# Modulation vectors of a two-layer backbone: five chunks summed on VectorE, four chunks moved to layer 1

## The chip, the cores and the metric

The kernel runs on one core of one Trainium2 chip. The metric is the device time of one execution in microseconds; before the change it is 2871.11 us (median of 3 runs, 2866.96 to 2872.5).

## What is computed

Two layers work on 1024 latent tokens of width 1024, with 256 context tokens beside them. Every layer is steered by modulation vectors that come from a conditioning vector:

```python
s_lat = jax.nn.silu(c)
s_ctx = jax.nn.silu(c_ctx)
for layer in range(DEPTH):
    mod   = (s_lat @ ada_w[layer] + ada_b[layer])[:, None, :]
    mod_c = s_ctx @ ada_w[layer] + ada_b[layer]
    sh1, sc1, g1, sh2, sc2, g2 = jnp.split(mod, N_MOD, axis=-1)          # latents
    csh1, csc1, cg1, csh2, csc2, cg2 = jnp.split(mod_c, N_MOD, axis=-1)  # context
    h   = modulate(x, norm1_g[layer], sh1, sc1)
    h_c = modulate(ctx, norm1_g[layer], csh1, csc1)
    # layer 0: Fourier mixing and spatial gating; layer 1: neighbourhood attention
    x = x + g1 * y
    x = x + g2 * conv_ffn(modulate(x, norm2_g[layer], sh2, sc2), ...)
    # the same for ctx in layer 0 only
```

`ada_w[layer]` is 1024 x 6144 in float32. The text calls one of its twelve blocks of 1024 columns a chunk, (layer, j) with j = 0 to 5: 4 MB of weights, multiplied by one or two vectors of 1024 numbers (the streams: latents and context). Layer 1 returns the latents only, so its chunks j = 2 to 5 are needed for the latents alone; (1,0) and (1,1) are needed for both.

## The kernel before, in words

**Order of the work.** A startup computes chunks (0,1) and (0,0). The even mixer follows: twelve projections of the normed input with `even_w_in` (method `even`, helper `go`), first four for the gating values and four for the gating units, then four for the Fourier part. Then eight projections with `even_w_out` (from L1617), the ConvFFN of layer 0, the 24 projections with `odd_w_qkv` (method `qkv`, from L1105), attention, its output projection, and the ConvFFN of layer 1. A projection of 1280 columns is 8 k-steps; each k-step is three passes (a float32 product is split into high and low parts) of three matmuls, 512, 512 and 256 columns wide (L556).

**Modulation by matmuls.** `ada` (from L634) works on a chunk: for each of 8 k it loads two tiles of 128 x 512 weights (L642) into a rotation of six tiles `adaw`, and issues four matmuls (L644). The silu vectors of both streams, padded to 32 columns, are the stationary operand; four column strips of the array hold four column blocks of 256. After k = 7 VectorE copies the sums out of PSUM (L649), two transposes (L652) turn them into columns, and VectorE adds the bias (L656). `gains` (L667) makes 1 + scale times the norm's gain for j = 1 and 4.

**Modulation by sums on VectorE.** `ada_sums` (from L670) is for the latents alone: a tile of weights 128 x 512 is multiplied by a per-partition scalar of `sT` and added to an accumulator (L684 for the first k, L686 for the other seven), two halves to a chunk, two k to one load of 512 KB (L680). What is left, a sum over the partitions, is eight matmuls with a column of ones (L692), each two instructions in the profile, and one addition of the bias (L694).

**What sets the order.** Both are generators. Each `next` traces one step; hooks call it at chosen k-steps of a projection, so that a step stands in the program between two k-steps. The framework then schedules the whole program at build time: on each engine it takes the first instruction in program order that it holds to be ready. On the chip each engine runs its list in that order and waits where an operand is not there. The loads of weights go through SyncE's queue (SP), also in order.

**Where the chunks stand.** In `even`, `go(10)` takes 10 steps, `go(11)` 8 and each of `go(4)` to `go(7)` 8: chunks (0,2) to (0,5), (1,1), (1,0), all by `ada`. In the projections with `even_w_out`, a hook at every k-step takes a step of (1,2) to (1,5) by `ada_sums`; accumulator and loads share four tiles of tag `wd`. The `qkv` projections have hooks of their own: `todo` holds the head norms and transposes of the projection before, placed at k-steps 1, 3, 5 and 7, or at 2.

Of the kernel before, what the change touches and what calls it, by code (L numbers as in the profile page):

```python
# [12 lines left out]
ALU = mybir.AluOpType  # L13
# [493 lines left out]
class Net:  # L507
# [77 lines left out]
    def setup(self, pool):  # L585
# [20 lines left out]
        self.gs = self.t(cp, [P, 2, 2, 2, KD], "gs")  # L606

        def early():
# [61 lines left out]
    def ada_sums(self, layer, j, room):  # L670


        nc, a = self.nc, self.a
        acc = room()
        for half in range(2):
            x = acc[:, half * 512:half * 512 + 512]
            lo = j * D + half * 512
            for k in range(0, KD, 2):
                w = room().rearrange("p (t n) -> p t n", t=2)
                nc.sync.dma_start(w, a["ada_w"][layer, k * P:(k + 2) * P, lo:lo + 512].rearrange("(t p) n -> p t n", p=P))  # L680
                for i in range(2):
                    c = self.sT[:, k + i, 0:1]
                    if k + i == 0:
                        nc.vector.tensor_scalar(x, w[:, i], c, None, ALU.mult)  # L684
                    else:
                        nc.vector.scalar_tensor_tensor(x, w[:, i], c, x, ALU.mult, ALU.add)  # L686
                yield

        def rest():
            tr = self.t(self.ps, [P, 512], "pq")  # L690
            for e in range(KD):
                nc.tensor.matmul(tr[:, e:e + 1], acc[:, e * P:(e + 1) * P], self.ones, start=True, stop=True)  # L692
            b = layer * 48 + j * 8
            nc.vector.scalar_tensor_tensor(self.mod[:, layer, 0, j, :], tr[:, 0:KD], float(D),  # L694
                                           self.adab[:, b:b + 8], ALU.mult, ALU.add)
            self.gains(layer, j, (0,))
        return rest
# [133 lines left out]
    def even(self, h, ada, spill, ws, hooks, close):  # L831
# [34 lines left out]
        with tc.tile_pool(name="sgu", bufs=1) as pool:  # L866
# [72 lines left out]
            for g in range(G):  # L939
# [4 lines left out]
                pl, pc = go(4 + g, hooks=hk, fill=8)[0]  # L944
# [927 lines left out]
```

## Time and profile before

One execution was profiled: 2865.27 us, of which the span from its first to its last instruction is 2863.4 us. All times below are of that execution.

| | us | share of the span |
|---|---|---|
| PE (TensorE matmuls) | 2747.1 | 96% |
| PEld (weight loads of TensorE) | 2507.2 | 88% |
| DVE (VectorE) | 2247.1 | 78% |
| ACT (ScalarE) | 1375.3 | 48% |
| POOL (GpSimd) | 917.9 | 32% |

Stages that the text speaks of, by time from the span's start: `go(11)` and `go(4)` to `go(7)` from 106.5 to 236.6 us; the Fourier projections to about 361 us; the projections with `even_w_out`, in which modulation is summed, from 361 to 455 us; the `qkv` projections from 1410 to 1756 us, most of them in 1455 to 1755 us.

A row of the timeline gives start, duration, engine, line, operation and operands, the number of merged instructions, and in brackets the idle time of the engine before it and who ended it. A row of the stages gives a stretch and for each engine its busy time and, in parentheses, its instructions; then the granted TensorE clock, the share of the DMA engines, and GB/s. A line L686 is line 686 of the kernel before. A matmul's end is modelled, so the starts of weight loads (PEld), which are issued in the order of the matmuls, show the pace of TensorE best.

### The profile page before, as it was taken

How to read it: one execution, taken by the hardware profiler on the slowest of the kernel's cores; microseconds unless marked ns; L12 is line 12 of the kernel's file. 1: busy time of each engine (PE TensorE's matmuls, PEld its weight loads, DVE VectorE, ACT ScalarE, POOL GpSimd, SP SyncE). 2: the span in 40 equal slices, each digit the busy share in tenths (PEclk: the TensorE clock that was granted, in tenths of full speed). 3: DMA queues.
4: the chain of work that ended last, by engine and by line, in shares of the span. 5: the costliest groups of instructions: out<-in, count | busy, mean ns of one | idle time of the engine just before them, and what ended most of it. 6: DMA issues, size and time to landing. Idle time of an engine off the chain costs nothing.

```text
span 2863.4 us, 46977 instructions
## 1 busy us (share of the span) xinstructions
PE 2747.1 (96%) x17978; PEld 2507.2 (88%) x17978; DVE 2247.1 (78%) x3680; ACT 1375.3 (48%) x2652; POOL 917.9 (32%) x840
## 2 busy tenths in 40 slices
PE   7999999899999899999999998999989999999998
PEld 4668878799999899999888887999778999789998
DVE  4233477988998998888876666999379999889997
ACT  4221314544444444444543334999255555545454
POOL 0600014532323742222221111444355343653331
PEclk9999999899999999999999999999999999999999
DMA  8764262322223222222043325775223333333333
GB/s 309 212 195 127 80 222 90 101 84 89 75 85 95 80 82 88 75 81 88 24 145 125 142 101 158 180 180 122 63 78 104 103 96 106 109 91 102 89 104 96
DMA packets 335882, 327.63 MB, mean 114 GB/s; under 512 B 16217, under 2 KB 264617, under 8 KB 335657
## 3 DMA queue, kind: packets, MB, share of 16 engines
q1 hardware_dynamic: 331509, 315.69, 36.6%
q0 software_dynamic: 3808, 7.87, 1.0%
q8 instruction: 142, 2.33, 0.3%
q10 hardware_dynamic: 340, 1.06, 0.1%
q14 instruction: 83, 0.68, 0.1%
HBM read 277.86 MB, written 46.71 MB: 113 GB/s over the span
## 4 chain that ended last, share of the span: by engine, by line
PE 68%; DVE 20%; DMA 4%; issue 4%; ACT 2%; POOL 1%; SPq 0%; POOLq 0%; DVEq 0%; ACTq 0%
PE pq L323 20%; PE pq L556 15%; PE pq L439 12%; PE ps L556 6%; DVE xl L449 3%; DVE wh L256 3%; DVE wq L256 3%; PE pq L644 2%; DVE wd L526 2%; PE ps L565 2%; DVE g L354 2%; PE st L1284 1%; PE tl L1317 1%; DVE hx L329 1%; DVE hs L526 1%
## 5 line engine op out<-in xcount | busy, mean ns | idle before, releaser
L439 PE MATMUL pq<-act,wd 128*128 128x320 f32 (+3 forms) x3696 | 615.4, 318 | 18.6 <-DVE hx L329 6.4
L323 PE MATMUL pq<-hs,wh 128*128 128x320 f32 (+3 forms) x4128 | 609.7, 300 | 20.0 <-ACT wh L251 7.8
L323 PEld LDWEIGHTS pq<-hs,wh 128*128 128x128 f32 x4128 | 579.6, 192 | 27.6 <-ACT wh L251 9.1
L439 PEld LDWEIGHTS pq<-act,wd 128*128 128x128 f32 x3696 | 549.7, 191 | 42.8 <-DVE hx L329 8.2
L323 PE MATMUL pq<-hs,wq 128*128 128x320 f32 (+3 forms) x3144 | 470.8, 297 | 12.6 <-ACT hx L332 7.3
L556 PE MATMUL pq<-hs,wh 128*128 128x512 f32 (+3 forms) x2100 | 465.5, 356 | 3.6 <-DVE hs L802 1.9
L323 PEld LDWEIGHTS pq<-hs,wq 128*128 128x128 f32 x3144 | 437.4, 189 | 20.5 <-ACT hx L332 10.8
L556 PEld LDWEIGHTS pq<-hs,wh 128*128 128x128 f32 x2100 | 362.7, 191 | 77.5 <-issue 6.2
L248 POOL TENSOR_TENSOR ws<-wr 128x512 f32<-128x512 f32 x88 | 133.2, 1513 | 629.3 <-DMA wr<-in_ffn_w_up_dram 493.4
L449 DVE SCALAR_TENSOR_TENSOR xl<-pq,mod,xl 128x320 f32<-128x320 f32 (+5 forms) x616 | 296.1, 513 | 11.0 <-PE pq L439 10.9
L556 PE MATMUL ps<-hs,wh 128*128 128x512 f32 x840 | 242.5, 408 | 4.4 <-ACT hs L799 1.7
L256 DVE TENSOR_TENSOR wq<-wr,wq 128x512 fp32r<-128x512 f32 x246 | 226.0, 933 | 25.8 <-ACT wq L251 25.6
L332 ACT ACTIVATE hx<-pq 128x320 f32<-128x320 f32 (+3 forms) x292 | 119.2, 408 | 220.6 <-PE pq L323 214.0
L251 ACT ACTIVATE wh<-ws 128x512 fp32r<-128x512 f32 x172 | 108.3, 629 | 195.8 <-PE pq L323 173.3
L259 POOL TENSOR_TENSOR wr<-ws,wr 128x512 f32<-128x512 f32 x88 | 121.2, 1378 | 196.4 <-DVE wh L256 177.2
L556 PEld LDWEIGHTS ps<-hs,wh 128*128 128x128 f32 x840 | 143.1, 192 | 42.6 <-issue 14.4
L251 ACT ACTIVATE wq<-wr 128x512 fp32r<-128x512 f32 x262 | 162.8, 622 | 30.0 <-POOL wr L258 15.8
L329 DVE TENSOR_TENSOR hx<-hx,pq 128x320 f32<-128x320 f32 (+3 forms) x304 | 134.7, 447 | 50.1 <-PE pq L323 32.3
L256 DVE TENSOR_TENSOR wh<-ws,wh 128x512 fp32r<-128x512 f32 x172 | 157.3, 914 | 9.8 <-ACT wh L251 5.9
L1084 DVE RECIPROCAL hsq<-hsq 128x512 f32<-128x512 f32 (+1 forms) x40 | 121.1, 3030 | 53.0 <-ACT hsq L1083 52.1
L526 DVE TENSOR_TENSOR wd<-wrd,wd 128x512 fp32r<-128x512 f32 x176 | 145.3, 860 | 0.3 <-ACT wd L525 0.3
L251 ACT ACTIVATE wh<-wr 128x512 fp32r<-128x512 f32 x172 | 107.6, 625 | 76.0 <-POOL wr L259 42.4
(312 smaller groups left out, 4380.9 us busy)
## 6 DMA issues: line engine op xcount, KB each, us to landing
wr<-in_ffn_w_up_dram SPq DMA_DIRECT2D x176, 512.0 KB, 4.6
wrd<-in_ffn_w_down_dram SPq DMA_DIRECT2D x88, 512.0 KB, 3.6
adaw<-in_ada_w_dram SPq DMA_DIRECT2D x128, 256.0 KB, 3.5
wd<-in_ada_w_dram SPq DMA_DIRECT2D x32, 512.0 KB, 4.8
wr<-in_odd_w_qkv_dram SPq DMA_DIRECT2D x24, 512.0 KB, 3.7
vd<-kvs SPq DMA_DIRECT2D x8, 1280.0 KB
v<-vd SPq DMA_DIRECT2D x16, 640.0 KB
kd<-kvs SPq DMA_DIRECT2D x8, 1280.0 KB, 4.6
```

The source lines that it names most:

```text
L248: op(raw["S1"], raw["A10"], raw["A11"], ALU.add)
L251: nc.scalar.activation(slots[name][:, 0], raw[name], AF.Copy)
L256: e.tensor_tensor(slots[name][:, 1], x, f32(slots[name][:, 0]), ALU.subtract)
L259: op(x, raw["S1"], x, ALU.subtract)
L323: nc.tensor.matmul(o, w[wn][:, wp, k], self.part(s, bn, k, sp), start=(onto is None and k == 0 and i == 0), stop=(k == 3 and i == 2), skip ...
L329: nc.vector.tensor_tensor(o, x, y, ALU.add)
L332: nc.scalar.activation(o, x, AF.Copy)
L439: nc.tensor.matmul(pd, self.wds[j][i][:, wp, d % 4], self.acts[f][:, sp, lo:lo + m], start=(i == 0 and pi == 0), stop=(i == len(fs) - 1 an ...
L449: nc.vector.scalar_tensor_tensor(x, pd[:, a - lo:b - lo], net.mod[:, self.layer, st, 5, d:d + 1], x, ALU.mult, ALU.add)
L526: return (e or self.nc.vector).tensor_tensor(l, src, f32(h), ALU.subtract)
L556: nc.tensor.matmul(o, w(wp, k), s(k, sp), start=(ki == 0 and pi == 0), stop=(ki == len(order) - 1 and pi == 2))
L1084: nc.vector.reciprocal(r, r)
```

## The change

- `setup` keeps a dense copy `sc` of the two silu vectors in the constants' pool, from which the scalars are taken.
- `ada_sums` now takes a list of streams and a width n. Per part of n columns it keeps one accumulator for each stream; every k is a load of its own (128 x n), used by one instruction per stream. It yields after every second k, and after the last k once more with a function that issues the ones-matmuls and the bias of that part.
- `ada_chain` runs several chunks in a row and calls that function `wait` steps after it was given; all uses have wait=1, so in the step in which it is given.
- Even mixer: (0,2) stays with `ada`; (0,3), (0,4), (0,5) go through `ada_chain`, both streams, n = 512, with two of the six `adaw` tiles as accumulators and four for the loads. `go(10)` takes 9 steps, `go(11)` and `go(4)` to `go(7)` 6 each.
- Projections with `even_w_out`: (1,1), (1,0), both streams, n = 512, accumulators from the three `wq` tiles, loads from the four `wd` tiles, one step at k-steps 0, 2, 4 and 6.
- `qkv`: (1,2) to (1,5), latents alone, n = 256, one accumulator and two load tiles, one step at k-steps 0, 2, 4, 6 (0, 3, 4, 6 where `todo` stands at 2).

```diff
+            nc.vector.tensor_copy(self.sc, self.sT[:, :, 0:2])
...
-    def ada_sums(self, layer, j, room):
+    def ada_sums(self, layer, j, room, streams, n):
         nc, a = self.nc, self.a
+        m = n // P
+        for part in range(D // n):
+            acc = [room("acc", n) for _ in streams]
+            lo = j * D + part * n
+            for k in range(KD):
+                w = room("w", n)
+                nc.sync.dma_start(w, a["ada_w"][layer, k * P:(k + 1) * P, lo:lo + n])
+                for i, s in enumerate(streams):
+                    c = self.sc[:, k, s:s + 1]
+                    if k == 0:
+                        nc.vector.tensor_scalar(acc[i], w, c, None, ALU.mult)
                     else:
+                        nc.vector.scalar_tensor_tensor(acc[i], w, c, acc[i], ALU.mult, ALU.add)
+                if k % 2:
+                    yield None
+
+            def left(part=part, acc=acc):
+                tr = self.t(self.ps, [P, 512], "pq")
+                b = layer * 48 + j * 8 + part * m
+                for i, s in enumerate(streams):
+                    for e in range(m):
+                        nc.tensor.matmul(tr[:, m * i + e:m * i + e + 1], acc[i][:, e * P:(e + 1) * P], self.ones,
+                                         start=True, stop=True)
+                for i, s in enumerate(streams):
+                    nc.vector.scalar_tensor_tensor(self.mod[:, layer, s, j, part * m:part * m + m], tr[:, m * i:m * i + m],
+                                                   float(D), self.adab[:, b:b + m], ALU.mult, ALU.add)
+                if part == D // n - 1:
+                    self.gains(layer, j, streams)
+            yield left
+
+    def ada_chain(self, chunks, room, n=512, wait=3):
+        late = []
+        for layer, j, streams in chunks:
+            for left in self.ada_sums(layer, j, room, streams, n):
+                if left is not None:
+                    late.append([wait, left])
+                for x in late:
+                    x[0] -= 1
+                while late and late[0][0] <= 0:
+                    late.pop(0)[1]()
                 yield
+        for _, left in late:
+            left()
...
-            r = go(10, ws=ws, hooks={1: r0, 4: r1}, fill=10)[0]
+            r = go(10, ws=ws, hooks={1: r0, 4: r1}, fill=9)[0]
-            r = go(11, hooks={2: r2}, fill=8)[0]
+            r = go(11, hooks={2: r2}, fill=6)[0]
-                pl, pc = go(4 + g, hooks=hk, fill=8)[0]
+                pl, pc = go(4 + g, hooks=hk, fill=6)[0]
...
+        more = self.ada_chain([(1, j, (0,)) for j in (2, 3, 4, 5)], lambda what, n: self.t(pool, [P, n], "adx" + what, bufs=2 if what == "w" else 1), 256, 1)
+
         def hooks():
...
+            res.update({i: lambda: next(more, None) for i in ((0, 3, 4, 6) if 2 in res else (0, 2, 4, 6))})
...
+            def mixed():
+                yield from self.ada(0, 2, room)
+                accs, ws = rooms[:2], rooms[2:]
+                def other(what, n):
+                    t = accs if what == "acc" else ws
+                    t.append(t.pop(0))
+                    return t[-1]
+                yield from self.ada_chain([(0, j, (0, 1)) for j in (3, 4, 5)], other, wait=1)
+            f, b, work = self.even(h, mixed(), spill, w, hooks, mstack.close)
...
+                    more = self.ada_chain([(1, 1, (0, 1)), (1, 0, (0, 1))], lambda what, n: (
+                        self.t(fp, [P, D], "wq", bufs=3) if what == "acc" else self.t(fp, [P, D], "wd", bufs=4))[:, :n], wait=1)
+                    hooks = {i: lambda: next(more, None) for i in (0, 2, 4, 6)}
```

More of the change, by code (lines that the diff above doesn't have):

```diff
@@ L606, in setup @@
         self.gs = self.t(cp, [P, 2, 2, 2, KD], "gs")
+        self.sc = self.t(cp, [P, KD, 2], "sc")
         def early():
@@ L951, in even @@
                 nc.vector.tensor_tensor(b[g][1], b[g][1], u[:, NL:], ALU.mult)
+            for _ in ada:
+                pass
         ws = [self.weights(w_in[:, g * P:(g + 1) * P]) for g in range(2)]
@@ L1191, in qkv @@
             f()
+        for _ in more:
+            pass
     def bias_setup(self, pool):
@@ L1551, in room @@
             def room():
-                return self.t(mp, [P, 512], "adaw", bufs=6)
+                rooms.append(rooms.pop(0))
+                return rooms[-1]
+            rooms = [self.t(mp, [P, 512], f"adaw{i}") for i in range(6)]
             first = self.ada(0, 1, room)
@@ L1582, in spill @@
                 late()
-            def rest(chunks, room):
-                left = []
-                for layer, j in chunks:
-                    if layer == 0 or j < 2:
-                        yield from self.ada(layer, j, room)
-                    else:
-                        one = self.ada_sums(layer, j, room)
-                        for i in range(KD):
-                            next(one)
-                            if i == 3:
-                                while left:
-                                    left.pop()()
-                            yield
-                        try:
-                            next(one)
-                        except StopIteration as e:
-                            left.append(e.value)
-                for fn in left:
-                    fn()
-            chunks = [(0, j) for j in (2, 3, 4, 5)] + [(1, j) for j in (1, 0, 2, 3, 4, 5)]
-            f, b, work = self.even(h, rest(chunks[:6], room), spill, w, hooks, mstack.close)
+            def mixed():
[7 more added lines that the diff above has]
+            f, b, work = self.even(h, mixed(), spill, w, hooks, mstack.close)
             y = {}
@@ L1647, in run @@
                     fp = fstack.enter_context(pool(name="ffn0", bufs=1))
-                    more = rest(chunks[6:], lambda: self.t(fp, [P, D], "wd", bufs=4))
-                    hooks = {i: lambda: next(more, None) for i in range(KD)}
+                    more = self.ada_chain([(1, 1, (0, 1)), (1, 0, (0, 1))], lambda what, n: (
+                        self.t(fp, [P, D], "wq", bufs=3) if what == "acc" else self.t(fp, [P, D], "wd", bufs=4))[:, :n], wait=1)
+                    hooks = {i: lambda: next(more, None) for i in (0, 2, 4, 6)}
                     ffn = Ffn(self, 0, (xl, xc), [t for k in order[:7] for t in y[k]], fp)
```

21 lines of the change are left out of this document (removed).

## The prediction

> **What bounds the kernel now.** I read the table of stages first, then TensorE's weight loads in the timeline, then the waits, then the instruction groups that the change touches.
>
> ```profile
> core 0: us, PE busy (x) PEld busy (x) DVE busy (x) ACT busy (x) POOL busy (x), PEclk, DMA share, GB/s
> 106.50:236.60 130.10, 130.10 (x839) 84.81 (x838) 37.50 (x61) 24.57 (x33) 27.74 (x48) 1.00 0.63 190
> 361.00:455.00 94.00, 85.74 (x443) 72.13 (x441) 73.91 (x96) 18.04 (x27) 21.18 (x14) 0.96 0.64 209
> 1455.00:1755.00 300.00, 299.03 (x1511) 251.34 (x1511) 198.10 (x160) 113.94 (x202) 42.39 (x36) 1.00 0.38 131
> ```
>
> These are the three stages that the change touches. In the even mixer (first row) TensorE is busy all 130.10 us while VectorE is busy 37.50. In the projections of layer 1 (last row) it is busy 299.03 of 300, VectorE 198.10. Only among the `even_w_out` projections does TensorE leave 8.3 of 94 us open, with VectorE at 73.91. So in the first and third stage a TensorE instruction less is time less, and one more is time more, as long as VectorE keeps up.
>
> A busy TensorE can hide waits, so I look at what a modulation step costs there.
>
> ```profile
> 108.90 0.14 PEld L644 LDWEIGHTS pq<-adaw,sT 128*32 128x32 f32 x4 [0.36 <-ACT wh L525]
> ...
> 122.37 0.19 PEld L556 LDWEIGHTS pq<-hs,wh 128*128 128x128 f32 x1 [0.41 <-issue]
> ...
> 123.70 0.19 PEld L556 LDWEIGHTS pq<-hs,wh 128*128 128x128 f32 x1 [0.41 <-issue]
> ...
> 216.17 0.16 PEld L644 LDWEIGHTS pq<-adaw,sT 128*32 128x32 f32 x8 [0.25 <-issue]
> 216.74 0.30 PEld L556 LDWEIGHTS ps<-hs,wh 128*128 128x128 f32 x2 [0.41 <-issue]
> 217.08 0.19 PEld L556 LDWEIGHTS pq<-hs,wh 128*128 128x128 f32 x1
> 217.32 0.30 PEld L556 LDWEIGHTS ps<-hs,wh 128*128 128x128 f32 x2
> ...
> 218.68 0.16 PEld L644 LDWEIGHTS pq<-adaw,sT 128*32 128x32 f32 x8 [0.25 <-issue]
> ...
> 228.72 0.16 PEld L644 LDWEIGHTS pq<-adaw,sT 128*32 128x32 f32 x8 [0.25 <-issue]
> ```
>
> One pass of a projection takes 217.32 - 216.74 = 0.58 us, a k-step of three passes 1.75. With a modulation step it takes 218.68 - 216.17 = 2.51, so a group of L644 costs 0.76. Where the scheduler splits a step in two groups of four, one pass and one such group take 123.70 - 122.37 = 1.33, so half a step costs 0.75 as well. From the row at 108.90 to that at 228.72 I count 57 groups (40 steps, 17 of them split).
>
> **The change part by part.**
>
> (a) Even mixer, TensorE. Away go 57 groups x 0.75 = 42.8 us, and five pairs of transposes.
>
> ```profile
> L652 PE MATMUL pq<-ident,adaw x16: 270/272/329, 26.7 to 234.6; 128*128 128x128 f32 x16
> L692 PE MATMUL pq<-ones,wd x64: 164/250/272, 380.2 to 452.0; 128*128 128x1 f32 x64
> 399.77 1.05 PE L692 MATMUL pq<-ones,wd 128*128 128x1 f32 x8 [1.95 <-DVE wd L686]
> 400.69 0.70 PE L556 MATMUL ps<-hs,wh 128*128 128x512 f32 x2
> ...
> 408.02 1.05 PE L692 MATMUL pq<-ones,wd 128*128 128x1 f32 x8 [1.26 <-DVE wd L686]
> ```
>
> A pair of 0.27 us, overlapped in part, I take at 0.4: together 45 us. New are the ones-matmuls. Four chunks of one stream have 64 instructions, 16 each; eight take 400.69 - 399.77 = 0.92 us, 0.115 each. Three chunks of two streams are 96, 11 us. If TensorE goes on setting the pace, the stage shortens by 45 - 11 = 34 us, to 96.
>
> (b) Even mixer, VectorE. The sums run in 512 columns; their price stands in the later stage.
>
> ```profile
> L686 DVE SCALAR_TENSOR_TENSOR wd<-wd,sT,wd x56: 740/752/1768, 362.4 to 450.3; 128x512 f32<-128x512 f32 x56
> L680 SPq DMA_DIRECT2D wd<-in_ada_w_dram x32: 367/368/462, 357.9 to 444.6; - x32
> L684 DVE TENSOR_SCALAR wd<-wd,sT x8: 480/486/943, 361.8 to 443.3; 128x512 f32<-128x512 f32 x8
> ...
> 106.50:236.60 130.10, 2.13 (x5) 1.00 0.63 190
> ...
> 106.50:236.60 130.10, 1.41 (x12) 1.00 0.63 190
> ```
>
> Three chunks are 6 parts x 2 streams x (0.486 + 7 x 0.752) = 69 us. The copies (L649, 2.13) and bias additions (L656, 1.41; the last two rows) go, so VectorE has 37.5 - 3.5 + 69 = 103, against 96 on TensorE. VectorE is then the longer by 7. Some of that can run on into the Fourier projections, but the framework prefers what stands earlier in the program, which are the sums; the gate and the eviction of the mixing matmuls, for which TensorE waits, stand behind them. I charge 8 us, the excess and a first load to wait for: -26. Loads fall from 20 to 12 MB here; nothing is charged for SP.
>
> (c) `even_w_out`. Work on VectorE stays: before 4 x 2 parts x 8 operations on one stream, now 2 x 2 x 8 x 2. TensorE keeps its 64 instructions. What can change are the waits.
>
> ```profile
> DVE wd L686 <- DMA wd<-in_ada_w_dram: 13.4, 8, 2.8
> PEld pq L692 <- DVE wd L686: 8.5, 4, 3.3
> ...
> DVE wd L684 <- DMA wd<-in_ada_w_dram: 6.6, 4, 2.9
> ...
> 408.00:413.00 5.00, 4.98 (x21) 4.31 (x22) 2.17 (x4) 0.00 (x0) 0.00 (x0) 0.67 0.67 198
> ...
> adaw<-in_ada_w_dram SPq DMA_DIRECT2D x128, 256.0 KB, 3.5
> wd<-in_ada_w_dram SPq DMA_DIRECT2D x32, 512.0 KB, 4.8
> ```
>
> VectorE stood still for loads for 13.4 + 6.6 = 20 us, and TensorE for VectorE 8.5 us in 4 waits, with the next projection queued behind the ones-matmuls. After the wait that ended at 408.02 the clock stood at 0.67 for 5 us: 1.65 us lost, and 0.96 over 94 us is 3.8 in all. Loads are halved (a load of 256 KB landed in 3.5 us, one of 512 KB in 4.8), and accumulators no longer take load tiles: VectorE should wait less. But the ones-matmuls come one step after the last sum, not four. Bounds: all waits gone, -12; twice as long, +12. I take -3, nearer to no change.
>
> The Trainium skill, TensorE: Matmul & The Clock Gate, "HAM oscillation", asks for no TensorE gap over about 3.4 us, and by it the short waits here would leave the clock alone; the trace disagrees, since 1.26 us before 408.02 and 1.95 before 399.77 were enough. By that rule 3.8 us fewer would be at stake.
>
> (d) Layer 1. TensorE gets 64 ones-matmuls, 64 x 0.115 = 7.4 us, nothing hides them. VectorE gets 16 parts of eight operations of 256 columns.
>
> ```profile
> L794 DVE SCALAR_TENSOR_TENSOR wq<-xc,gs,act 128x256 f32<-128x256 f32 x8 | 3.7, 480 | 0.0
> ...
> L1077 POOL TENSOR_TENSOR hsp<-hsq,hsp 128x512 fp32r<-128x512 f32 (+1 forms) x36 | 42.4, 1186 | 252.4 <-ACT hsq L1076 252.4
> ...
> 376.28 4.67 POOL L722 TENSOR_TENSOR act<-act,wrd 128x512 f32<-128x512 f32 x3 [133.32 <-ACT wrd L720]
> ...
> 376.50 1.63 DVE L686 SCALAR_TENSOR_TENSOR wd<-wd,sT,wd 128x512 f32<-128x512 f32 x1
> ```
>
> At 0.48 (the first, a scalar product, at 0.28 as an estimate from half of L684's) that is 58 us, so VectorE rises from 198 to 256 of 307: it still has room. The 128 loads of 128 KB issue in 0.368 us each, 47 us of SP's queue; a load that waits there for one of only two tiles holds up the next `odd_w_qkv` weights and the stores behind it, and a sum that waits for its load holds up the head norms on VectorE, to which the PSUM tiles of the next projection are tied. No row shows that chain; it costs nothing if loads land early, and 36 us in the case worked out below. A step is due every two k-steps, 3.5 us, and a 256 KB load lands in 3.5, so I stay near the low end: 16 handovers of 0.3 us, 5. Sum +12.
>
> Beside GpSimd one sum took 1.63 instead of 0.752 us (last two rows). The sums fill 58 of 307 us, so of 36 GpSimd operations some seven meet one, 6 us more on VectorE, inside its room. The Trainium skill, SBUF — State Buffer, "SBUF: two separate sides", speaks against the change here: an operation with two SBUF inputs and a GpSimd operation exclude each other for the whole instruction, which a matmul never meets. The trace agrees by the 0.88 us added; with 1.2 us for each of the seven the sum would be 8 us on VectorE rather than 6.
>
> (e) The copy `sc` runs in the startup, about 0.2 us of VectorE, under the first loads.
>
> Sum: -26 - 3 + 12 = -17 us on the profiled 2865.3, hence 2848. The median of the runs is 2871.1, 5.8 above that execution; I set the change against the median: **2854 us**.
>
> **The rivals.**
>
> *TensorE keeps the pace everywhere.* VectorE's excess runs on into the Fourier projections, and handovers cost nothing: -34 - 3 + 7.4 = -30, 2841; with all waits of (c) gone too, 2832. For it: VectorE filled only 37.5 of 130.10 us, and much of the sums' work can be done before it is due. Against it: 103 against 96.
>
> *The handover eats the gain.* A part has one accumulator for each stream: its first product waits until TensorE has read the old sums, and TensorE's ones-matmuls wait, in order, for the last new one. Two us of idle VectorE at each of 6 parts in (b) is 12 us in a stage that VectorE bounds: -14 - 3 + 12 = -5, 2866, no measurable change. The four waits of (c), 2.1 us each, speak for it.
>
> *Slower: VectorE waits for small loads in layer 1.* In (c) it waited 20 us for 32 loads, 0.63 each. At that price 128 loads cost 80 us, and 198 + 58 + 80 = 336 us of VectorE no longer fit into 300: the stage grows by 36, and the whole is -26 - 3 + 36 = +7, 2878. It decides from (307 - 256) / 128 = 0.4 us per load; two tiles instead of four speak for it, loads of a quarter of the size against it.
>
> That the groups' 0.75 us do not come free is hardly open: nothing but TensorE's own order stands behind them.
>
> **How the numbers follow.** My forecast gets 0.50, the first rival 0.13, the handover 0.16, the slower case 0.21. A measurement of this kernel can tell about 0.2%, 5.7 us, from no change. Forecast and first rival are faster, and so is a sixth of the handover case, 0.65; the rest of it 0.14; slower 0.21. The range reaches from the first rival with the waits gone, 2832, to just past the slower case, 2880.
>
> **What would show it.** Right: no L644 after about 106 us; the even stage some 26 us shorter with VectorE near full; 64 ones-matmuls in each later stage; the stretch of layer 1 about 12 us longer at a clock of 1.00. Wrong: the even stage down by 34 (first rival), idle VectorE ended by TensorE's ones-matmuls there (second), or sums that wait over 0.4 us per load in layer 1 and projections that start late behind head norms (third).

## The result and the profile after

The changed kernel takes **2905.54 us** (median of 4 runs, 2901.9 to 2911.98) beside 2870.31 for the kernel before on the same chip: 1.0135 times as long, with a 95% interval of 1.0119 to 1.0151. It is slower by 1.35%, outside the range of 2832 to 2880. All times and ratios here leave out one execution, of a later kernel, that took 6717 us, more than twice any other. The profiled execution of the changed kernel took 2905.19 us with a span of 2903.2.

The first part of the page after says how the engines share it: TensorE is busy for 10 us less than before, VectorE for 112 us more, in a span that is 39.8 us longer.

```profile
span 2903.2 us, 47171 instructions
...
PE 2737.0 (94%) x17808; PEld 2528.1 (87%) x17808; DVE 2359.6 (81%) x3922; ACT 1376.9 (47%) x2652; POOL 921.1 (32%) x840
```

To see where the time went I compared the same events in both traces, in us from the span's start (the two rows on the FFN and on `qkv` go by the first weight load):

| event | before | after | difference |
|---|---|---|---|
| first eviction of the Fourier projections (ScalarE) | 250.57 | 234.98 | -15.6 |
| first matmul of the FFN of layer 0 | 485.68 | 456.43 | -29.3 |
| first `qkv` projection of layer 1 | 1399.47 | 1370.43 | -29.0 |
| first matmul of attention | 1761.28 | 1807.31 | +46.0 |
| end | 2863.4 | 2903.2 | +39.8 |

So the even mixer gave 15.6 us and the `even_w_out` projections 13.7; the `qkv` projections took 75.1 back. The last 6 us lie in attention and the FFN of layer 1, which the change does not touch.

The table of stages of the kernel after has three rows that answer to those of before (even mixer, `even_w_out`, layer 1 from its first projection to attention):

```profile
core 0: us, PE busy (x) PEld busy (x) DVE busy (x) ACT busy (x) POOL busy (x), PEclk, DMA share, GB/s
105.30:221.00 115.70, 106.76 (x592) 93.79 (x591) 94.90 (x147) 26.98 (x35) 30.84 (x51) 0.91 0.51 151
...
345.40:425.70 80.30, 80.30 (x437) 68.96 (x437) 70.52 (x100) 17.29 (x26) 20.31 (x14) 1.00 0.47 145
...
1370.40:1807.30 436.90, 378.22 (x1840) 314.87 (x1839) 301.52 (x389) 144.91 (x265) 63.36 (x56) 0.92 0.40 132
```

and the third stage of the kernel before, now with the same two ends:

```profile
1399.50:1761.30 361.80, 353.07 (x1777) 295.57 (x1776) 245.52 (x242) 144.90 (x264) 62.39 (x56) 0.99 0.33 113
```

In layer 1 no engine is full: TensorE is busy 378 of 437 us and VectorE 302. The 75.1 us are 50.0 in which TensorE stands open (436.90 - 378.22 = 58.7 instead of 8.7) and 25.1 in which it is busy for longer, of which 64 ones-matmuls are 7.4 by the prediction's price; the rest goes with a clock of 0.92 instead of 0.99. Some 6 of the 75 us are not the moved chunks': the kernel without them (first experiment) takes 368.2 us for this stage. Who ended the open time is in the waits of that stage:

```profile
DVE adxacc L689 <- DMA adxw<-in_ada_w_dram: 69.7, 36, 5.1
PE pq L698 <- DVE adxacc L689: 34.4, 7, 9.5
...
PE pq L1108 <- POOL hsp L1103: 11.5, 2, 10.1
...
DVE adxacc L687 <- DMA adxw<-in_ada_w_dram: 3.8, 1, 3.8
```

TensorE stood 34.4 us in 7 of the 16 parts because the ones-matmuls (L698) wait for the last sum, and VectorE stood 73.5 us because the sums wait for loads. Another 11.5 us of TensorE's waits are at L1108, a head norm's matmul that waits for GpSimd (see "What is open"). The longest of the seven waits in the timeline:

```profile
1666.20 1.00 DVE L689 SCALAR_TENSOR_TENSOR adxacc<-adxw,sc,adxacc 128x256 f32<-128x256 f32 x2
1666.31 0.38 SPq L530 DMA_DIRECT2D wr<-in_odd_w_qkv_dram  x1
1666.80 12.89 SPq L683 DMA_DIRECT2D adxw<-in_ada_w_dram  x8
1671.85 0.48 DVE L689 SCALAR_TENSOR_TENSOR adxacc<-adxw,sc,adxacc 128x256 f32<-128x256 f32 x1 [4.64 <-DMA adxw<-in_ada_w_dram]
1672.45 0.93 PEld L698 LDWEIGHTS pq<-ones,adxacc 128*128 128x128 f32 x4 [9.92 <-issue]
1672.48 0.99 PE L698 MATMUL pq<-ones,adxacc 128*128 128x1 f32 x4 [9.52 <-DVE adxacc L689]
1673.26 5.46 PEld L556 LDWEIGHTS pq<-hs,wh 128*128 128x128 f32 x18
```

Read it from the bottom. The projection (L556) goes on at 1673.26; TensorE had nothing for 9.52 us, although that projection's operands were there, because four tiny matmuls stand ahead of it in its list. They wait for the last sum at 1671.85, and that sum for its load, for 4.64 us: SP put the load out only at 1666.80, after the first of the two sums at 1666.20 had freed a tile. The load then took some 5 us to land and not the 2.1 that is the median of these loads; the DMA engines were full meanwhile:

```profile
1666.80:1671.90 5.10, 0.00 (x0) 0.00 (x0) 0.46 (x2) 0.00 (x0) 0.00 (x0) 0.56 0.96 337
```

This part is not typical. In five of the seven, 24.1 of the 34.4 us, the last sum starts right behind other work of VectorE, with no idle time before it. The second longest is such a one:

```profile
1475.48 0.48 DVE L689 SCALAR_TENSOR_TENSOR adxacc<-adxw,sc,adxacc 128x256 f32<-128x256 f32 x1 [2.27 <-DMA adxw<-in_ada_w_dram]
1475.88 3.34 DVE L1110 RECIPROCAL hsq<-hsq 128x512 f32<-128x512 f32 x1
1481.85 0.83 DVE L689 SCALAR_TENSOR_TENSOR adxacc<-adxw,sc,adxacc 128x256 f32<-128x256 f32 x1
1482.82 0.98 PE L698 MATMUL pq<-ones,adxacc 128*128 128x1 f32 x4 [7.53 <-DVE adxacc L689]
```

Here a load held up an earlier sum, and head norms, with a reciprocal of 3.34 us among them, stand on VectorE between that sum and the last. So the sums come late by loads and by VectorE's own order together.

### The profile page after: what moved, and what is told of

Same layout as the page of the kernel before. It is cut to its first block, busy times and chain, and to the rows that moved or that the text cites. A ratio compares the mean times of both kernels' runs of the same rounds, so it can differ in the third digit from the quotient of the medians.

```text
span 2903.2 us, 47171 instructions
## 1 busy us (share of the span) xinstructions
PE 2737.0 (94%) x17808; PEld 2528.1 (87%) x17808; DVE 2359.6 (81%) x3922; ACT 1376.9 (47%) x2652; POOL 921.1 (32%) x840
## 4 chain that ended last, share of the span: by engine, by line
PE 58%; DVE 21%; ACT 8%; issue 6%; DMA 5%; POOL 1%; SPq 0%; DVEq 0%; POOLq 0%; ACTq 0%
PE pq L323 20%; PE pq L439 13%; PE pq L556 12%; PE ps L556 7%; DVE xl L449 3%; ACT t L1336 3%; DVE wh L256 3%; DVE wq L256 2%; DMA adxw<-in_ada_w_dram 2%; DVE wd L526 2%; PE ps L565 2%; DVE g L354 1%; DVE hx L329 1%; DVE hs L526 1%; DVE g L341 1%
## 5 line engine op out<-in xcount | busy, mean ns | idle before, releaser
L323 PE MATMUL pq<-hs,wq 128*128 128x320 f32 (+3 forms) x3144 | 475.2, 299 | 19.9 <-ACT hx L332 10.6
L556 PE MATMUL pq<-hs,wh 128*128 128x512 f32 (+3 forms) x2100 | 469.2, 364 | 4.3 <-DVE hs L826 1.9
L556 PEld LDWEIGHTS pq<-hs,wh 128*128 128x128 f32 x2100 | 370.3, 198 | 71.9 <-DVE hs L826 3.0
L248 POOL TENSOR_TENSOR ws<-wr 128x512 f32<-128x512 f32 x88 | 133.0, 1511 | 615.1 <-DMA wr<-in_ffn_w_up_dram 475.4
L556 PE MATMUL ps<-hs,wh 128*128 128x512 f32 x840 | 231.4, 405 | 4.5 <-ACT ut L972 2.9
L556 PEld LDWEIGHTS ps<-hs,wh 128*128 128x128 f32 x840 | 147.6, 193 | 34.8 <-ACT ut L972 3.4
L251 ACT ACTIVATE wq<-wr 128x512 fp32r<-128x512 f32 x262 | 162.8, 622 | 23.9 <-POOL wr L258 16.1
L1103 POOL TENSOR_TENSOR hsp<-hsq,hsp 128x512 fp32r<-128x512 f32 (+1 forms) x40 | 49.0, 1228 | 334.2 <-ACT hsq L1102 321.9
L262 POOL TENSOR_TENSOR ws<-wr 128x512 f32<-128x512 f32 x88 | 119.5, 1359 | 62.1 <-DVE wh L256 54.8
```

The lines of the kernel that those rows point to most:

```text
L248: op(raw["S1"], raw["A10"], raw["A11"], ALU.add)
L251: nc.scalar.activation(slots[name][:, 0], raw[name], AF.Copy)
L262: op(x, raw["A01"], raw["S2"], ALU.subtract)
L323: nc.tensor.matmul(o, w[wn][:, wp, k], self.part(s, bn, k, sp), start=(onto is None and k == 0 and i == 0), stop=(k == 3 and i == 2), skip ...
L556: nc.tensor.matmul(o, w(wp, k), s(k, sp), start=(ki == 0 and pi == 0), stop=(ki == len(order) - 1 and pi == 2))
```

## The experiments

Two theories stood first. **L** (loads): each load waits for one of two tiles, the last sum of a part is late, and TensorE, in order, stands behind it; with the clock that falls afterwards this is the cost. **V** (VectorE's work): the sums delay the head norms, whatever the loads do. A third, **Q**, is SP's queue, in which 128 loads hold up weights and stores. "The stage" below is from the first `qkv` projection to the first matmul of attention in the profiled execution: 361.8 us before, 436.9 after. The kernel before ran beside each group, at 2865.5 to 2868.8 us; ratios are to it.

**Layer 1's part taken apart.** The first kernel leaves chunks (1,2) to (1,5) out (they are zeros).

```diff
-        more = self.ada_chain([(1, j, (0,)) for j in (2, 3, 4, 5)], ..., 256, 1)
+        nc.vector.memset(self.mod[:, 1, 0, 2:6, :], 0.0)
+        self.gains(1, 4, (0,))
+        more = iter(())
```

> Leaves out chunks (1,2) to (1,5): no loads, sums or ones-matmuls in the projections of layer 1, and zeros stand for their modulation. Both other moves stay. All theories: the stage in layer 1 is as before the change, and the even mixer and the even_w_out projections keep what the changed kernel's trace shows (-15.6 and -13.7 us), so 2870 - 29 = 2841 us. If the time stays above 2860, the loss comes from something outside the moved chunks.

Measured: 2836.48 us, 0.9885 [0.9868, 0.9901]. The other two stages are worth 32 us against the kernel before beside it (2868.8), near the 29 of the trace, and layer 1's part alone costs 2905.5 - 2836.5 = 69 us.

The second has every sum of these chunks read one tile that is loaded once, so that one load is left in it:

```diff
-                w = room("w", n)
-                nc.sync.dma_start(w, a["ada_w"][layer, k * P:(k + 1) * P, lo:lo + n])
+                if n == 256 and self.fixed is not None:
+                    w = self.fixed
+                else:
+                    w = room("w", n)
+                    nc.sync.dma_start(w, a["ada_w"][layer, k * P:(k + 1) * P, lo:lo + n])
+                    if n == 256:
+                        self.fixed = w
```

> The sums of layer 1 all read one weight tile that is loaded once: the sums' 128 VectorE operations and the 64 ones-matmuls stay, 127 of 128 loads are left out, so the values of those chunks are not the reference's. Theory L (the sums wait for loads that go through two tiles, and TensorE waits in order for the last sum): without loads the stage grows only by ones-matmuls and short waits, 2841 + 8 to 17, so 2849 to 2858 us, and ones-matmuls wait under 1 us each. Theory V (58 us of sums are too much for VectorE beside the head norms and GpSimd): hardly better than the change, 2890 us or more. Theory Q (loads hold up weights and stores in the SP queue): like L, 2849 to 2858.

Measured: 2861.22 us, 0.9973 [0.9963, 0.9983]. It is 3 us above the bracket of L and Q and 29 below that of V.

The third keeps loads and sums and leaves out the ones-matmuls, with the bias behind them:

```diff
             def left(part=part, acc=acc):
+                if n == 256:
+                    return
```

> Loads and sums of layer 1 stay as in the change; the 64 ones-matmuls and the bias additions behind them are left out, and zeros stand for the modulation of those chunks. Theory L with the wait on TensorE as the price: TensorE no longer stands behind the last sum, so 36 us of waits, 7 us of matmuls and most of the clock loss go: 2845 to 2860 us. Theory V or Q: VectorE is as late and the queue as full as before, so projections still start late behind head norms or weights: 2885 us or more.

Measured: 2852.96 us, 0.9945 [0.993, 0.996]: inside L's bracket. The fourth is the complement, ones-matmuls on a tile that is filled once, without loads and sums:

```diff
+                if n == 256:
+                    if k % 2:
+                        yield None
+                    continue
                 w = room("w", n)
```

> The 64 ones-matmuls and bias additions of layer 1 stay but read one tile that is filled once; the loads and sums of those chunks are left out, so their values are not the reference's. All theories: 64 x 0.115 = 7 us of TensorE and nothing to wait for, 2841 + 7 to 10, so 2848 to 2851 us. If it costs over 20 us more than the kernel without layer 1's chunks, the ones-matmuls themselves (PSUM tile, place in the order) are the price and not what they wait for.

Measured: 2856.35 us, 0.9955 [0.9938, 0.9973]: a miss, 5 us above the bracket, and 19.9 above the kernel without these chunks, right at the 20 from which the ones-matmuls themselves were to count as the price. The four rows of the stage, in that order (nothing, no loads, no ones-matmuls, ones-matmuls alone):

```profile
1373.50:1741.70 368.20, 359.55 (x1776) 300.80 (x1775) 244.34 (x241) 144.98 (x263) 61.45 (x56) 0.97 0.32 111
```

```profile
1367.10:1755.30 388.20, 369.88 (x1841) 309.54 (x1840) 301.40 (x389) 144.61 (x265) 64.82 (x56) 0.95 0.31 106
```

```profile
1369.70:1743.20 373.50, 360.14 (x1776) 301.92 (x1775) 287.11 (x359) 144.06 (x263) 63.85 (x56) 0.95 0.46 152
```

```profile
1363.00:1747.00 384.00, 368.96 (x1842) 309.54 (x1841) 244.43 (x259) 143.66 (x263) 62.26 (x56) 0.96 0.31 107
```

Loads and sums together, with nothing on TensorE waiting for them, lengthen the stage by 5.3 us (373.5 - 368.2), although VectorE still waits 34.5 us for loads. Ones-matmuls alone lengthen it by 15.8, sums with ones-matmuls by 20.0. Only all three make 68.7. By the medians the three kernels cost 16.5, 19.9 and 24.7 us against 69; the 16.5 is larger than its 5.3 because that kernel's time behind the start of attention, where nothing was changed, was 11.7 us longer (1109.2 against 1097.5), and this is not explained. By either measure it is no sum of costs but a meeting of two: late sums, and TensorE behind them. V falls as the main cost: in the second kernel VectorE's 301.40 us of work are all there, with head norms and sums, and TensorE's waits at the ones-matmuls come to 0.4 us.

**Is it the queue?** The loads of layer 1 go to ScalarE's queue:

```diff
-                nc.sync.dma_start(w, a["ada_w"][layer, k * P:(k + 1) * P, lo:lo + n])
+                (nc.scalar if n == 256 else nc.sync).dma_start(w, ...)
```

> The change, with the 128 loads of layer 1 issued by ScalarE's queue instead of SyncE's. Theory Q (the loads are late because they stand in the SP queue behind weights and stores that wait): they come in time, 2850 to 2870 us. Theory T (the loads are late because only two tiles exist, so each load starts only when a sum two places ahead has ended, and lands 2.1 us later): no better, 2890 us or more, and ScalarE, which now waits for tiles in its own order, can make it worse.

Measured: 2911.02 us, 1.0149 [1.0128, 1.0169]. Another queue saves nothing, and the sums still wait 60.1 us for loads, so Q falls. What is left of L is called **T** from here on: the two tiles make the last sum late. T does not say how much of that is loads that land late because the DMA engines are full, as in the timeline above; no run was made for it.

**More tiles.** Beside the attention's first tiles there was no room for eight load tiles, so these tiles and loads moved behind the last projection:

```diff
-... "adx" + what, bufs=2 if what == "w" else 1), 256, 1)
+... "adx" + what, bufs=8 if what == "w" else 1), 256, 1)
...
-            with tc.using_default_side("right"):
-                self.att_begin(att.enter_context(pool(name="att0", bufs=1)))
...
-                if pr == 1:
-                    first.append(self.att_load(0))
+                pass
             with pool(name="qkv", bufs=1) as kp:
                 self.qkv(h, kp, ready, begun)
+            with tc.using_default_side("right"):
+                self.att_begin(att.enter_context(pool(name="att0", bufs=1)))
+            first.append(self.att_load(0))
```

> The change with eight load tiles instead of two in layer 1. To make room, the tiles of attention are allocated and its first head is loaded after the projections of layer 1 instead of beside them, which by itself should cost attention's start 5 to 10 us. Theory T: all eight loads of a part can be in flight, sums no longer wait, and the stage costs about what the ones-matmuls cost without loads: 2836 + 20 + 5 to 10, 2860 to 2880 us, with under 15 us of VectorE waiting for loads. Theory Q: still late behind weights and stores, 2895 us or more.

Measured: 2872.32 us, 1.0018 [1.0005, 1.003]. Then, besides, two accumulators and the ones-matmuls three steps later (`bufs=8 if what == "w" else 2), 256, 3)`):

> As the kernel with eight load tiles, with two accumulators, and the ones-matmuls traced three steps after the last sum instead of in the next. If a place right behind the last sum is itself a cost (TensorE waits in order): 5 to 15 us less than with eight tiles alone, 2850 to 2870. If loads were the whole cause: the same as with eight tiles within 4 us.

Measured: 2862.31 us, 0.9978 [0.9967, 0.9988]. Both are inside their brackets, but the second not for the reason given: neither kernel has a wait at the ones-matmuls to lose. Of the 10 us between them, 6.0 are a wait for GpSimd at L1108 that only the first has. In the waits of the two kernels, from the stage's start until attention runs, what TensorE waits at L698 comes to 0.4 us at most, and the sums wait 4 to 5 us for loads instead of 73.5:

```profile
PE st L1315 <- issue: 20.9, 1, 20.9
...
DVE adxacc L687 <- DMA adxw<-in_ada_w_dram: 2.4, 1, 2.4
DVE adxacc L689 <- DMA adxw<-in_ada_w_dram: 1.7, 2, 1.5
```

```profile
PE st L1315 <- issue: 21.7, 1, 21.7
...
DVE adxacc L687 <- DMA adxw<-in_ada_w_dram: 2.9, 2, 2.4
DVE adxacc L689 <- DMA adxw<-in_ada_w_dram: 2.0, 2, 1.7
```

The first matmul of attention (L1315) now waits 21 us for loads that used to lie under the projections; I had expected 5 to 10. It hides what eight tiles give.

**Narrow tiles instead.** With parts of 128 columns, five load tiles and two accumulators take little more memory than the changed kernel's two and one of 256 (3.5 KB instead of 3 in each partition), and attention can stay where it was.

```diff
-... bufs=2 if what == "w" else 1), 256, 1)
+... bufs=5 if what == "w" else 2), 128, 3)
...
-            res.update({i: lambda: next(more, None) for i in ((0, 3, 4, 6) if 2 in res else (0, 2, 4, 6))})
-            return res
+            old = dict(res)
+            return {i: lambda i=i: (old[i]() if i in old else None, next(more, None)) for i in range(KD)}
```

> The layer-1 part of the changed kernel with parts of 128 columns instead of 256: the same memory then holds five load tiles and two accumulators instead of two and one, the ones-matmuls of a part come three steps after its last sum, and a step stands at every k-step of a qkv projection. The whole computation is done. Theory (what costs layer 1 its 70 us is two load tiles, so that the last sum of a part is late, and TensorE standing in order behind it, with the clock that falls after): with the handover loosened the stage loses most of that, 2850 to 2872 us as with eight tiles and the late ones-matmuls (2862), at an unchanged start of attention. Rival (VectorE's own work or the number of loads is what costs): the sums are now 256 instead of 128, of some 0.35 us, about 88 us of VectorE instead of 58, and 256 loads instead of 128, so the kernel stays at 2890 us or gets slower than the changed one (2905).

Measured: 2901.61 us, 1.0124 [1.0107, 1.014]: a miss for my theory as I had put it, and inside the rival's bracket of 2890 or more. Five tiles and a handover that is three steps later recovered 4 us. This run alone can't tell late loads from the twofold number of sums and loads. Its waits of the stage:

```profile
DVE adxacc L689 <- DMA adxw<-in_ada_w_dram: 29.3, 28, 4.1
PE pq L698 <- DVE adxacc L689: 29.1, 6, 9.7
...
DVE adxacc L687 <- DMA adxw<-in_ada_w_dram: 16.7, 9, 3.6
PEld pq L698 <- issue: 13.4, 1, 13.4
PE pq L698 <- DMA adxw<-in_ada_w_dram: 13.3, 1, 13.3
```

TensorE still stands 42.4 us at ones-matmuls (29.1 + 13.3). The number of tiles is thus not the measure. A load tile of this kernel is free again sooner, but a part also passes faster: from the first sum to the last it is 343.6 us for 32 parts, 10.7 us each, so five tiles reach 5/8 of that, 6.7 us, ahead. In the changed kernel it is 345.1 us for 16 parts, 21.6 each, of which two tiles reach 2/8, or 5.4 us; eight tiles reach a whole part, 16.3 us in the kernel with the late ones-matmuls. These are estimates from the traces. Measured load by load, from its issue to the start of the sum that reads it, the medians are 4.2 us in the changed kernel, 5.2 with five narrow tiles and 16.1 in the kernel with the late ones-matmuls. That the reach in time decides is argued from them, not shown by a run of its own. The stop of 13.3 us, at the first part, has a cause in SP's order, in the waits of its queue:

```profile
SPq L1247 <- DVE hx L826: 61.3, 1, 61.3
```

The load of the attention's mask (L1247) waits 61.3 us for memory, and the first modulation loads stand behind it.

**Tiles or the attention's loads?** The kernels with eight tiles had changed both. The control moves attention as they do and keeps two tiles and one accumulator.

> The changed kernel with its two load tiles and one accumulator kept, and only the attention's tiles and first loads moved behind the qkv projections, as they were in the kernels with eight tiles. Theory T (two tiles are what makes the last sum late): the stage stays as long as in the changed kernel and attention starts some 20 us later, 2900 to 2930 us. Rival S (the attention's first loads stand in SP's queue ahead of modulation loads, and moving them was what helped, not the tiles): 2865 to 2885 us, as with eight tiles (2872).

Measured: 2905.06 us, 1.0128 [1.0115, 1.0142], the time of the changed kernel. Attention starts 3 us later, not the 20 expected, and in the waits of the stage all is as it was:

```profile
DVE adxacc L689 <- DMA adxw<-in_ada_w_dram: 66.7, 36, 5.0
PE pq L698 <- DVE adxacc L689: 33.3, 7, 10.1
```

But this is no test of S. The edit moved the loads in the program only; with two tiles the memory was free, and the schedule put them where they had been. The first load of q in the changed kernel and in this one:

```profile
1443.96 0.52 SPq L1268 DMA_DIRECT2D q<-qd  x1
```

```profile
1446.07 0.52 SPq L1268 DMA_DIRECT2D q<-qd  x1
```

With eight tiles it was put out at 1764.9 us. What speaks against S is the time of the waits: in the changed kernel attention's first loads have all been put out by 1468 us, and 26.9 of the 34.4 us that TensorE waits at the ones-matmuls lie behind 1557 us. The eight tiles are thus the cause that is left; a run that moves only the loads was not made.

**The mended version.** Eight tiles, two accumulators, the late ones-matmuls, and five steps to a projection; the chunks are then done by the sixth head pair, and their memory goes to the attention's tiles.

```diff
+                self.adx = adx.enter_context(pool(name="adx", bufs=1))
...
-                if pr == 1:
+                if pr == 5:
+                    for _ in self.more:
+                        pass
+                    adx.close()
+                    with tc.using_default_side("right"):
+                        self.att_begin(att.enter_context(pool(name="att0", bufs=1)))
                     first.append(self.att_load(0))
```

> Eight load tiles, two accumulators, the ones-matmuls three steps later, five steps to a projection, so that the four chunks are done by the sixth of the eight head pairs; their memory is then given to the attention's tiles, whose first loads start there and not after the last projection. Theory T: no TensorE wait at a ones-matmul, as in the kernel with eight tiles and late ones-matmuls (2862), and attention starts without its pause of 22 us: 2838 to 2856 us, faster than the kernel before. Rival S (what counts is that the attention's loads are not among the modulation loads): they come after them here as well, so S expects the same; but by a rival that has VectorE's 58 us of sums as the cost, packing them into fewer projections makes it worse, 2865 us or more.

Measured: **2848.0 us**, 0.9931 [0.9919, 0.9943]: faster than both kernels. Its stage and the waits that matter in it:

```profile
1364.00:1744.00 380.00, 369.01 (x1841) 309.55 (x1840) 297.82 (x386) 144.57 (x263) 63.26 (x56) 0.96 0.46 152
```

```profile
DVE adxacc L687 <- DMA adxw<-in_ada_w_dram: 3.3, 3, 2.4
...
PE st L1316 <- DVE kvs L1172: 0.8, 1, 0.8
```

380 us instead of 436.9, with VectorE's 298 us of work as before: the same sums in fewer projections, so V falls here too. Against the kernel without these chunks they cost 11.8 us in the stage (380.0 - 368.2) and 11.5 by the medians (2848.0 - 2836.5), the +12 that I had forecast for two tiles.

**The `even_w_out` stage alone.** In the kernel before, only the loads and tiles were changed: (1,2) to (1,5) stay there for the latents alone, but with 256 KB to a load and accumulators of their own.

```diff
+        more = self.ada_chain([(1, j, (0,)) for j in (2, 3, 4, 5)], lambda what, n: (
+            self.t(fp, [P, D], "wq", bufs=3) if what == "acc" else self.t(fp, [P, D], "wd", bufs=4))[:, :n], wait=1)
```

> The kernel before, except that the sums of (1,2) to (1,5) among the even_w_out projections use the changed kernel's tiles: accumulators in their own tag, loads of 256 KB in four tiles, ones-matmuls in the next step. Even mixer and layer 1 as before the change. If the tiles and loads took away the waits of that stage: -12 to -14, 2855 to 2858 us. If it was the second stream (two sums for one load): under 4 us better than before, 2865 to 2870.

Measured: 2872.03 us, 1.0011 [0.9998, 1.0024]: no gain. The tiles and loads did not take the waits away, and the time is 2 us above the other bracket too. The waits of that stage:

```profile
DVE wq L689 <- DMA wd<-in_ada_w_dram: 15.1, 18, 2.9
PE pq L698 <- DVE wq L689: 8.7, 4, 3.3
```

On TensorE they are those of before (8.5 us in four waits). In the changed kernel the sums of that stage wait less, and no ones-matmul waits:

```profile
DVE wq L689 <- DMA wd<-in_ada_w_dram: 4.9, 4, 1.6
DVE wq L687 <- DMA wd<-in_ada_w_dram: 1.8, 1, 1.8
```

What differs most between the two is the second stream: every load now feeds two sums, and the stage moves 145 GB/s instead of 209. The steps differ as well, one in two k-steps instead of one in each, and no run has the second stream alone.

**The even mixer.** Chunks (1,2) to (1,5) left out as in the first experiment, and (0,3) back to matmuls, so that two chunks are summed on VectorE:

```diff
                 yield from self.ada(0, 2, room)
+                yield from self.ada(0, 3, room)
...
-                yield from self.ada_chain([(0, j, (0, 1)) for j in (3, 4, 5)], other, wait=1)
+                yield from self.ada_chain([(0, j, (0, 1)) for j in (4, 5)], other, wait=1)
```

> Chunks (1,2) to (1,5) left out (zeros, as in the kernel without the layer-1 part, 2836 us), and in the even mixer chunk (0,3) goes back to matmuls on TensorE, so that two chunks instead of three are summed on VectorE. Theory (VectorE bounds the even stage after the change, 103 us of work, and its sums run on into the Fourier projections): 23 us of VectorE go, TensorE gets back 8 steps of 0.75 or 1.5 us, some 9 to 12 us less about 4 of ones-matmuls; the stage is then at balance, 2828 to 2838 us. Rival (TensorE sets the pace there, VectorE hides): the chunk on TensorE costs its full 6 to 8 us, 2842 us or more.

Measured: 2836.2 us, 0.9892 [0.9878, 0.9906], inside the theory's bracket, and the same as with three chunks (2836.48). The stages until the first Fourier eviction, of the kernel with three chunks and of this one:

```profile
105.30:241.00 135.70, 127.66 (x681) 112.31 (x680) 99.78 (x155) 27.02 (x35) 36.11 (x59) 0.87 0.49 145
```

```profile
105.30:229.30 124.00, 119.55 (x710) 97.61 (x709) 78.28 (x122) 26.88 (x35) 33.96 (x57) 0.99 0.52 150
```

With more instructions on TensorE (710 against 681) the stage is 11.7 us shorter in these executions, at a clock of 0.99 instead of 0.87. The totals are equal because the FFN of layer 1 was 10.4 us longer here (770.0 against 759.6); nothing was changed in it, and that difference is not explained.

Both edits together, two chunks in the even mixer and parts of 128 columns in layer 1:

> Both edits together, the whole computation done: two chunks on VectorE in the even mixer, layer 1 in parts of 128 columns with five load tiles and two accumulators. If the two stages are independent, its time is that of the kernel with parts of 128 columns plus what the even edit gave against the kernel without the layer-1 part (between -8 and +8 us): 2842 to 2880 us.

Measured: 2889.55 us, 1.0079 [1.0066, 1.0092], above a bracket that rested on 2850 to 2872 for the parts of 128 columns. It is 12 us below that kernel, more than the 8 expected at most. And the same edit on the mended version:

> The kernel with eight tiles and the attention's first loads under the projections (2848 us), with chunk (0,3) of the even mixer back on matmuls, so that two chunks are summed on VectorE there; the whole computation is done. Theory (the even stage loses most of its gain to short TensorE waits and to the clock that halves after them, 14 to 34 us at half clock with three chunks, 3.4 with two): the time at half clock in the even stage stays under 8 us, and the whole is 0 to 8 us faster, 2840 to 2848 us. If the third chunk on VectorE is worth its matmuls: 2850 to 2856 us.

Measured: 2847.23 us, 0.9926 [0.9906, 0.9945], the same as 2848.0. So the third chunk on VectorE is worth nothing in two comparisons and costs 12 us in one; why they differ stays open.

**The even mixer's part alone**, with everything else where it was before:

```diff
                 yield from self.ada_chain([(0, j, (0, 1)) for j in (3, 4, 5)], other, wait=1)
+                for j in (1, 0):
+                    yield from self.ada(1, j, room)
```

> The even mixer's part of the change alone, the whole computation done: chunks (0,3), (0,4), (0,5) are summed on VectorE there, (0,2), (1,1), (1,0) go by matmuls, (1,2) to (1,5) stay among the even_w_out projections, with the new tiles and loads. Nothing is added to layer 1. Theory: with two more chunks of matmuls than the changed kernel TensorE has about 114 us in the even stage and VectorE 103, so VectorE does not bound it: -45 x 3/5 + 11 = -16 us there, and nothing elsewhere: 2850 to 2858 us. If the sums cost more than their time where they stand (handovers, the clock), 2860 us or more.

Measured: 2883.4 us, 1.0056 [1.0041, 1.0071]: the expectation failed, and the other bracket, 2860 or more, held. The stage ends at 250.1 us, where it ended before, so that three chunks on VectorE gained nothing in it:

```profile
105.30:250.00 144.70, 131.40 (x758) 107.72 (x759) 102.09 (x162) 27.12 (x35) 35.57 (x52) 0.91 0.56 171
```

TensorE stands open for 13.3 us, 7.9 of them in one wait of the mixing matmuls for their operand, and the clock is at 0.91. The Fourier projections then took 89 us instead of 72, with their matmuls in another order; why the scheduler put them so I did not follow.

## Why the prediction was wrong

**The bound of the kernel: right.** TensorE sets the pace, and its order of instructions is what a wait costs.

**(a) TensorE in the even mixer: right.** No modulation matmul (L646 in the new numbering) starts after 103 us. By the first row of the stages after, 115.70 us less 8.94 open, less 0.09 x 115.7 = 10.4 for the clock, is 96.4: the 96 of the forecast.

**(b) VectorE in the even mixer: the term was mis-sized, and for the wrong reason.** Forecast -26, measured -15.6. I charged 8 us for VectorE's excess, but VectorE was busy 94.90 of 115.70 us. What took the gain were short waits of TensorE and the clock after them, 8.94 + 10.4 = 19.3. Of the 8.94, one wait of 3.97 is ones-matmuls behind the last sum, as the handover case had it; the rest is three waits of 1.0 to 2.1 us for ScalarE, which no case had. None had a term for the clock here, although I had priced the clock in (c).

**(c) `even_w_out`: the size missed, the reason wrong.** Forecast -3, measured -13.7, a little past my bound for all waits gone. I gave smaller loads and separate accumulators as the reason; the kernel that had only these kept the waits. That the second stream removed them, because it makes two sums of each load, is argued and not shown. One reading in (c) was wrong: after the wait of 1.95 us that ended at 399.77 the clock did not fall. It stood at 1.00 until the next wait had ended:

```profile
399.80:408.00 8.20, 6.96 (x38) 5.80 (x38) 5.13 (x8) 1.06 (x1) 0.00 (x0) 1.00 0.75 244
```

**(d) Layer 1: the step that failed.** "A step is due every two k-steps, 3.5 us, and a 256 KB load lands in 3.5, so I stay near the low end: 16 handovers of 0.3 us, 5. Sum +12." Measured +75 in the trace, +69 by the kernel without it. It failed in two ways. I compared a load's landing with the distance of steps, but with two tiles a load isn't put out before a sum frees its tile, and that sum stands between head norms on VectorE, whose reciprocal takes 3.34 us. And I priced a late sum by VectorE's time, which had room, and not by TensorE's, which stands in order behind it: in place of 16 handovers of 0.3 us the trace has 34.4 us in seven, up to 9.52 each, and the clock at 0.92 where I had put nothing.

**The slower rival had the place and a good part of the mechanism.** It forecast 80 us of VectorE waiting for loads, 0.63 each, with a threshold of 0.4; the trace has 73.5 us, 0.57 each. But it took the time to be lost where VectorE's work no longer fits, +36. VectorE's work and waits are 301.5 + 73.5 = 375 us, 13 more than the 361.8 of before; that account gives 13 and not 75. The experiments show the true price: where no matmul waits for the sums, loads and sums cost 5.3 us of the stage, and where one does the part costs 69.

**(e)** `sc` shows no cost that stands out: `go(10)` ended 1.2 us earlier than before (105.3 against 106.5), with a step less in it.

**What is open.** In the kernels with ones-matmuls one step after the sums, a head norm's matmul early in the stage (L1108, between 1430 and 1445 us) waits for GpSimd, 6.0 us with ones-matmuls alone and 10.1 in the changed kernel; where ones-matmuls are left out or come three steps later it is 1.3 us or nothing. I did not find out how they are linked. Nor is it known why the time behind the start of attention, with the same program there, differs from kernel to kernel: 1095.9 us in the changed kernel, 1109.9 with the loads in ScalarE's queue.

## What to carry to other kernels

Before moving work to an idle engine, ask which instruction of the busy engine will wait for its last result, and what stands behind that instruction in order: idle share on the new engine is no cover for it. Give such a chain enough load tiles to run through the bursts of whatever shares its engine, a second accumulator, and a consumer that comes some steps later; the same four chunks cost 69 us with two tiles and 12 with eight, a second accumulator and the later consumer. And price a short wait of TensorE with the clock that follows it, not with its length alone.

## What the runs showed of the hardware

The clock can fall after waits much shorter than I would have thought harmful in a stage that is otherwise full. In the even mixer after the change, the timeline of weight loads has two waits in a row, and the row of the stages that follows has a clock of 0.81 over 27 us:

```profile
140.01 0.30 PEld L565 LDWEIGHTS ps<-ws,vs 128*128 128x128 f32 x2 [2.39 <-ACT vs L525]
142.35 0.93 PEld L556 LDWEIGHTS ps<-hs,wh 128*128 128x128 f32 x3 [2.04 <-ACT ut L972]
```

```profile
141.30:168.40 27.10, 26.05 (x140) 22.94 (x140) 20.42 (x30) 3.49 (x4) 4.90 (x10) 0.81 0.45 129
```

Waits of 2.39 and 2.04 us were followed by some 5 us of lost clock (0.19 x 27.1). The Trainium skill, TensorE: Matmul & The Clock Gate, "HAM oscillation", speaks of gaps over about 3.4 us; both are shorter, so the trace disagrees here, as it did before the change with the wait of 1.26 us that ended at 408.02 and a clock of 0.67. Not every such wait does it: after 1.95 us at 399.77 the clock stayed at 1.00.

On VectorE a reciprocal is far longer than a sum of the same width, so a sum that stands between head norms in VectorE's order comes late. From the groups of the kernel with parts of 128 columns:

```profile
L1110 DVE RECIPROCAL hsq<-hsq 128x512 f32<-128x512 f32 x32 | 107.1, 3346 | 16.2 <-ACT hsq L1109 16.1
L689 DVE SCALAR_TENSOR_TENSOR adxacc<-adxw,sc,adxacc 128x128 f32<-128x128 f32 x224 | 83.3, 378 | 33.7 <-DMA adxw<-in_ada_w_dram 29.3 <-DVE adxacc L689 0.2
```

A reciprocal of 512 columns took 3.35 us in the mean, 4.5 times a sum of that width (0.75). A sum of a quarter of the columns isn't a quarter of the price either: 0.378 us for 128, 0.48 for 256 (the timeline above) and 0.75 for 512.
